# Fourteen gate tiles by Strassen's method in a hybrid attention layer on one Trainium2 core

## The chip, the core and the metric

The kernel runs on one core of a Trainium2 chip. The engines are TensorE (PE in the profile, PEld for its weight loads), VectorE (DVE), ScalarE (ACT), GpSimd (POOL) and SyncE (SP), which issues the DMA transfers here. The metric is device time in microseconds, the median over runs. Each kernel has beside it one profiled execution, from which all rows of the profile come.

## The reference

A decoder layer over 2048 positions of width 1024, with 16 meta positions ahead. One input projection makes queries, keys and values of two attention branches and four gates; both attentions are gated, projected, merged under two sigmoid gates and added to the residual.

```python
xn = rms_norm(h, norm_gain[l])
proj = xn @ w_in[l]
sb_q, sb_k, sb_v, sw_q, sw_k, sw_v, sb_z, sw_z, g_sb, g_sw = jnp.split(proj, offsets, axis=-1)
...
y_sb = (o_sb * jax.nn.silu(sb_z)) @ w_branch_sb[l]
y_sw = (o_sw * jax.nn.silu(sw_z)) @ w_branch_swa[l]
merged = jax.nn.sigmoid(g_sb) * y_sb + jax.nn.sigmoid(g_sw) * y_sw
h = h + merged @ w_out[l]
return rms_norm(h, final_norm_gain)[:, BLOCK:]
```

The change concerns `sigmoid(g_sb)` and `sigmoid(g_sw)`: 8 + 8 column tiles of 128 of the input projection.

## The kernel before

The sequence is stored in reverse and cut into four groups of 512 positions. Two halves are worked one after the other: groups 2 and 3, then groups 0 and 1. For each group the normed input lies transposed in SBUF as eight slices of 128 rows, each in two parts: `xh`, rounded to fp32r, and `xl`, the remainder. Weights are split in the same way (`weights`: `wh` by one operation of 128x1024, `wl` by a second one; both on GpSimd in the stages that matter here). A product of full accuracy is then three fp32r matmuls a slice: high by high, high by low, low by high (`gemm`, L400 to L402). So a column tile of one group is 24 matmuls of 128x128 by 128x512 into one PSUM bank.

The order on TensorE is written out by hand (`manual_schedule`); on the other engines a planner places the instructions, and each engine works its own in order. SyncE's queue is in order too. Split weights are written to DRAM in the first half and read back in the second, where they need no splitting.

A half runs through these stages:

- Projections of the sliding-window branch, with that attention woven in (`window`).
- Stick-breaking attention (`stick`), woven with gate tiles. `weave` takes the gate tiles' slices one by one and lets the attention have a share of TensorE's time after each (`ratio`). A row step makes 128 queries by up to 512 keys: two matmuls (L836), a sigmoid on ScalarE (L840), for the diagonal blocks a mask on GpSimd (L845), and a running product on VectorE (`row`, the scan of L847). Five steps later (`LT`) `turn` transposes the row on TensorE (L858) and splits it (L111 on ScalarE, L112 on VectorE), and `values` multiplies it with the values (L884). In the first half there are 8 heads, each with group 3 (4 rows) and group 2 (8 rows). With each head and group, `row` loads the queries into two buffers each of tags q1 and q2, and in the first half also a block of `x` into a buffer of tag q2, whose squares ScalarE sums for the norm of the second half (L823).
- The gate tiles that are left.

The list `gts` holds 28 gates in order: 4 for the stick-breaking z, 8 for the sliding-window z (both with silu), 8 for `g_sb`, 8 for `g_sw` (sigmoid alone, L555). Each tile's result goes to DRAM (`zs`, `zw`, `gs`, `gw`). In the first half gts 3 runs ahead of the attention, gts 4 to 24 are woven with it, and gts 25 to 27 follow, group by group. Among these last, `prep` normalises the first group of the second half into the buffers of `xh[2]` and `xl[2]`; that is possible as soon as group 2 has had its last product.

```python
rest = 25 if half == 0 else 23
cost_sb = 8 * sum(4 * (4 - g) for g in groups) * 1.31 + 16 * 0.75
ratio = cost_sb / ((rest - 4) * 10.4)
weave(tiles_by_tile(gts[4:rest], groups), side, ratio)
drain(side)
```

Buffers that matter: `tmp` (nine of 128x512), `ring_x` (four), `raw` (two weight tiles as loaded), `wh` and `wl` (three each), and PSUM tags g, z and t with two banks each.

Of the kernel before, what the change touches and what calls it, by code (L numbers as in the profile page):

```python
# [8 lines left out]
F32R = mybir.dt.float32r  # L9
I32 = mybir.dt.int32  # L10
AF = mybir.ActivationFunctionType
ALU = mybir.AluOpType
# [4 lines left out]
P = 128  # L17
D = 1024
KT = D // P
SEQ = 2048  # L20
NM = 16
GT = 512
# [10 lines left out]
ULAG = 3  # L33
AB = 6
QW = 6.0
C_SBQ, C_SBK, C_SBV, C_SWQ, C_SWK, C_SWV, C_SBZ, C_SWZ, C_GSB, C_GSW = (
    0, 512, 1024, 1536, 2560, 2688, 2816, 3328, 4352, 5376)


def f32(ap):  # L40
    return ap.bitcast(F32)
# [3 lines left out]
def tile_kernel(ctx, tc, x, xt, meta, metat, gain, w_in, w_sb, w_sw, w_out, sinks, fgain,  # L45
# [6 lines left out]
    V, A, G, T = nc.vector, nc.scalar, nc.gpsimd, nc.tensor  # L52

    def DMA(dst, src):
        nc.sync.dma_start(*(t.bitcast(F32) if t.dtype == F32R else t for t in (dst, src)))
# [6 lines left out]
    def ps(tag):  # L62
        return pp.tile([P, 512], F32, tag=tag, name="ps_" + tag, bufs={"g": 2, "z": 2, "zm": 1, "t": 2, "o": 1}[tag])
# [28 lines left out]
    gs = [[dram(f"gs{p}_{g}", [P, GT]) for g in range(4)] for p in range(8)]  # L92
    gw = [[dram(f"gw{p}_{g}", [P, GT]) for g in range(4)] for p in range(8)]
# [55 lines left out]
    def drain(*gens):  # L149
        for _ in chain(*gens):  # L150
            pass
# [6 lines left out]
    def load(c0, w=w_in):  # L158
        raw = wp.tile([P, KT, P], F32, tag="raw", name="raw", bufs=2)[:, :w.shape[2], :]
        DMA(raw, w[c0 // P])  # L160
        return raw

    def weights(c0, w=w_in, raw=None, split=split):

        if c0 in ready:
            return ready.pop(c0)
        n = w.shape[2]
        wh, wl = (wp.tile([P, KT, P], F32R, tag=t, name=t, bufs=3)[:, :n, :] for t in ("wh", "wl"))
        key = w.name, c0
        if key in kept:  # L170
            for t, k in zip((wh, wl), kept[key]):
                DMA(t, k)
            return wh, wl
        raw = load(c0, w) if raw is None else raw
        split(wh, wl, raw)
        kept[key] = [dram(f"{t}_{w.name}_{c0}", [P, n, P], F32R) for t in "hl"]
        for t, k in zip((wh, wl), kept[key]):
            if put_off is None:
                DMA(k, t)
            else:  # L180
                put_off.append((k, t))
        return wh, wl
# [145 lines left out]
    xh, xl = {}, {}  # L328

    def tmp(dt=F32, rows=P):  # L330
        return tp.tile([rows, GT], dt, tag="tmp", name="tmp", bufs=9)

    def ring_x(dt=F32):
        return tp.tile([P, GT], dt, tag="xs", name="xs", bufs=XS)
# [43 lines left out]
    def prep(g, rs):  # L378

        x_tiles(g, g % 2)  # L380
        rb = scale_rows(rs)
        for k in range(KT):
            t = ring_x()
            DMA(t, xt[g, k])
            drain(normal(g, k, t, rb))
# [175 lines left out]
    def tiles_by_tile(makes, groups, meta=False):  # L561
        for mk in makes:
            w, use, wants = mk()
            for n, g in enumerate(reversed(groups) if wants == "back" else groups):
                yield from lagged(col_tile(w, g, use, meta and wants and n == 0))

    def by_group(ts, groups):
        for g in groups:
            for w, use, _ in ts:
                yield from lagged(col_tile(w, g, use))  # L570
# [204 lines left out]
    def stick(groups, bp, sums_of={}):  # L775
# [120 lines left out]
        for s in range(n + LT + 3):  # L896
# [12 lines left out]
            while av_todo and turned[0] < s - 1:  # L909
                del turned[0]  # L910
                yield values()


    sbt = [lambda p=p, f=f: f(p) for f, p in ((sb_k, 0), (sb_k, 1), (sb_q, 0), (sb_v, 0), (sb_v, 1), (sb_q, 1),
                                              (sb_k, 2), (sb_v, 2), (sb_q, 2), (sb_k, 3), (sb_v, 3), (sb_q, 3))]
    gts = ([lambda p=p: gate(C_SBZ + p * P, zs[p], True) for p in range(4)]
# [4 lines left out]
    halves = ([2, 3], [0, 1])  # L921
# [3 lines left out]
    with (tc.tile_pool(name="start", bufs=1, side="left") as bp,  # L925
# [54 lines left out]
        raw = load(C_SBK)  # L980
# [101 lines left out]
    for half, groups in enumerate(halves):  # L1082
        with tc.tile_pool(name=f"swa{half}", bufs=1, side="left") as sp:
            m = half == 0
            vsplit[0] = True
            if not m:
                ts = [mk() for mk in sbt[:3]]
                rs = rs1
            if not m:
                prep(groups[1], rs)  # L1090
                drain(by_group(ts, groups[:1]), by_group(ts, groups[1:]))
            if m:
                late_consts()
            sw_k, sw_v, sw_q, attend, ending = window(half, groups, sp)
            q = [[lambda p=p: sw_q(p) for p in (2 * s, 2 * s + 1)] for s in range(4)]
            steps = [(s, g) for s in range(4) for g in groups]
            if m:
                (wk, use_k, _), (wv, use_v, _), (wq, use_q, _) = sw_k(), sw_v(), sw_q(0)
                hold[0] = True
                drain(col_tile(wk, g0, use_k), col_tile(wv, g0, use_v), col_tile(wq, g0, use_q, bank="z"))  # L1100
                flush(waiting)
                drain(lagged(col_tile(wk, g1, use_k, True, "o", "t")))
                hold[0] = False
                meta_k = pending[:]
                del pending[:]
                drain(col_tile(wv, g1, use_v, True, "z", "t"))
                pending.append(lambda: flush(waiting))
                back = tp.tile([P, GT], F32, tag="rb", name="back", bufs=1)
                for i in range(2):
                    sums_back.append(back[:NM, i * P:(i + 1) * P])  # L1110
                    DMA(sums_back[i], msd[i])
                hand.close()
                vsplit[0] = False
                drain(tiles_by_tile(q[0][1:], groups[:1]))
                vsplit[0] = True
                late.extend(meta_k)
                pending.append(lambda: pending.extend(held))
            else:
                drain(tiles_by_tile([sw_k, sw_v], groups), tiles_by_tile(q[0], groups[:1]))
            drain(tiles_by_tile(sbt[3:4], groups, m))  # L1120
            main = chain(*[chain(tiles_by_tile(q[s], [g]), tiles_by_tile(sbt[3 + j:4 + j], groups, m))
                           for j, (s, g) in enumerate(steps) if j], tiles_by_tile([sbt[11], *gts[:3]], groups, m))
            side = attend()
            weave(main, side, 4 * 2.15 / 20.8 * SR)
            ending.append(1)
            drain(side)
            flush_all()
        with tc.tile_pool(name=f"sb{half}", bufs=1, side="left") as bp:
            vsplit[0] = False
            next_sums = {g: sums() for g in halves[1]} if half == 0 else {}  # L1130
            side = stick(groups, bp, next_sums)
            drain(tiles_by_tile(gts[3:4], groups))
            rest = 25 if half == 0 else 23
            cost_sb = 8 * sum(4 * (4 - g) for g in groups) * 1.31 + 16 * 0.75
            ratio = cost_sb / ((rest - 4) * 10.4)
            weave(tiles_by_tile(gts[4:rest], groups), side, ratio)
            drain(side)
            if half == 0:
                t, u = (bp.tile([P, GT], F32, tag="wh", name="sum", bufs=3)[:, :8] for _ in range(2))
                for n, ssq in enumerate(next_sums.values()):  # L1140
                    V.tensor_tensor(t[:, 4 * n:4 * n + 4], ssq[:, 0], ssq[:, 1], op=ALU.add)
                rs = tp.tile([P, 8], F32, tag="rs8", name="rs", bufs=1)
                rsqrt(rs, t, tp, t=u)
                rs0, rs1 = rs[:, :4], rs[:, 4:]
        if half == 0:
            ts = [mk() for mk in gts[rest:]]
            drain(by_group(ts, groups[:1]), by_group(ts[:1], groups[1:]))
            prep(halves[1][0], rs0)
            drain(by_group(ts[1:], groups[1:]))
        else:  # L1150
            ringl = rings()
            osw = {}
            todo = [(k, g) for g in halves[0] for k in range(8)]
            for mk in gts[rest:]:
                if mk is gts[-1]:
                    with tc.manual_schedule(engines={mybir.EngineType.Activation}):
                        drain(tiles_by_tile([mk], groups))
                        A.preload_act_table_set("natural_log_exp_and_others")
                else:
                    drain(tiles_by_tile([mk], groups))  # L1160
                for k, g in todo[:4]:
                    osw[k, g] = gated(ow, zw, k, g, ringl, tmp)
                del todo[:4]
            for k, g in todo:
                osw[k, g] = gated(ow, zw, k, g, ringl, tmp)
# [51 lines left out]
```

## Time and profile before

| | us |
|---|---|
| median of 3 runs (2173.67 to 2174.96) | 2173.68 |
| the profiled execution | 2175.12 |
| its span, first to last instruction | 2173.4 |
| TensorE busy in the span | 2147.3 |
| VectorE busy | 1360.6 |
| ScalarE busy | 1010.1 |
| GpSimd busy | 374.7 |

The profile's rows have line, engine, operation, output and inputs, shapes and count; then busy time and mean time of one; then idle time of the engine ahead of them and what ended it. The slices divide the span into 40 equal parts and give busy shares in tenths. Matmuls are pipelined, so a matmul's own duration is longer than the distance to the next one; distances are what count on TensorE.

### The profile page before, as it was taken

To read this page: it belongs to the slowest core of one execution; us is meant where nothing else is said; L and a number is where in the kernel's file an instruction comes from. 1 tells how busy PE (TensorE), PEld (TensorE's weight loads), DVE (VectorE), ACT (ScalarE), POOL (GpSimd) and SP (SyncE) were. 2 spreads that over 40 slices of the span, in tenths; PEclk is the share of its full clock that TensorE was granted. 3 is DMA by queue.
4 is the path that set the end of the run, shared out by engine and by line. 5 is a ranking of instruction groups with operands and counts; after the bars stand their busy time and mean duration, and the time that the engine had idled before them with its cause. 6 is when DMAs were issued, how large, how long until landed. Compare 5 with 4: busy or idle time off the path is not lost. (4 is left out here: it accounts for less than half of the span.)

```text
span 2173.4 us, 30334 instructions
## 1 busy us (share of the span) xinstructions
PE 2147.3 (99%) x10614; PEld 1764.0 (81%) x10614; DVE 1360.6 (63%) x2133; ACT 1010.1 (46%) x2344; POOL 374.7 (17%) x486
## 2 busy tenths in 40 slices
PE   8999999999999999999999999999999999999998
PEld 6788888888888888888877888888888888787886
DVE  7787875456555343877747888878774536453453
ACT  6677774344444324776744555555553202221121
POOL 2233343322232200232210000000000232000000
PEclk9999999999999999999999999999999999999999
DMA  9745445765565464444355433333324976467532
GB/s 333 284 173 194 175 165 206 251 197 196 170 196 192 157 216 155 146 148 156 133 171 150 124 122 112 115 108 97 117 86 135 349 276 205 164 218 271 154 97 87
DMA packets 162616, 380.41 MB, mean 175 GB/s; under 512 B 23168, under 2 KB 24960, under 8 KB 162464
## 3 DMA queue, kind: packets, MB, share of 16 engines
q1 hardware_dynamic: 162464, 378.48, 51.8%
q8 instruction: 84, 1.38, 0.3%
q14 instruction: 68, 0.56, 0.1%
HBM read 237.35 MB, written 140.98 MB: 174 GB/s over the span
## 5 line engine op out<-in xcount | busy, mean ns | idle before, releaser
L400 PE MATMUL ps_g<-xh,wh 128*128 128x512 f32 x1544 | 637.5, 413 | 7.7 <-ACT xh L934 6.8
L402 PE MATMUL ps_g<-xh,wl 128*128 128x512 f32 x1544 | 607.5, 393 | 1.0 <-DVE wl L108 1.0
L401 PE MATMUL ps_g<-xl,wh 128*128 128x512 f32 x1544 | 607.2, 393 | 0.0
L847 DVE TENSOR_TENSOR_SCAN row<-row 128x512 f32<-128x512 f32 (+2 forms) x320 | 371.2, 1162 | 167.0 <-POOL row L845 96.3
L402 PEld LDWEIGHTS ps_g<-xh,wl 128*128 128x128 f32 x1544 | 290.3, 188 | 66.9 <-DVE wl L108 1.9
L400 PEld LDWEIGHTS ps_g<-xh,wh 128*128 128x128 f32 x1544 | 291.7, 189 | 54.7 <-ACT xh L934 6.8
L401 PEld LDWEIGHTS ps_g<-xl,wh 128*128 128x128 f32 x1544 | 292.0, 189 | 43.7 <-DVE xl L935 1.3
L840 ACT ACTIVATE row<-ps_z 128x512 f32<-128x512 f32 (+1 forms) x320 | 171.9, 538 | 250.9 <-PE ps_z L836 207.9
L112 DVE SCALAR_TENSOR_TENSOR wtl<-ps_t,wth 128x512 fp32r<-128x512 f32 (+1 forms) x320 | 190.0, 594 | 47.3 <-ACT wth L111 45.8
L111 ACT ACTIVATE wth<-ps_t 128x512 fp32r<-128x512 f32 (+1 forms) x320 | 170.2, 532 | 91.1 <-PE ps_t L858 89.3
L836 PE MATMUL ps_z<-kt,q 128*128 128x512 f32 (+3 forms) x640 | 185.1, 370 | 0.3 <-ACT row L840 0.3
L858 PE MATMUL ps_t<-ident,row 128*128 128x128 f32 x1088 | 171.6, 273 | 1.2 <-DVE row L847 1.2
L858 PEld LDWEIGHTS ps_t<-ident,row 128*128 128x128 f32 x1088 | 135.9, 140 | 37.3 <-DVE row L847 1.7
L845 POOL TENSOR_SCALAR_AFFINE_SELECT row<-row 128x128 f32<-128x128 f32 x128 | 45.8, 359 | 620.0 <-ACT row L840 547.6
L836 PEld LDWEIGHTS ps_z<-kt,q 128*128 128x128 f32 x640 | 118.8, 188 | 26.4 <-ACT row L840 0.8
L884 PE MATMUL ps_o<-wth,vc 128*128 128x512 f32 (+1 forms) x320 | 125.8, 393 | 1.3 <-DVE tmp L889 1.1
L555 ACT ACTIVATE tmp<-ps_g 128x512 f32<-128x512 f32 x112 | 67.0, 598 | 121.3 <-PE ps_g L402 118.8
L107 POOL TENSOR_SCALAR wh<-raw 128x1024 fp32r<-128x1024 f32 (+1 forms) x63 | 65.8, 1045 | 331.3 <-PE ps_g L401 142.8
L701 ACT ACTIVATE sc<-sc,nm 128x129 f32<-128x129 f32 x256 | 100.0, 393 | 37.9 <-DVE nm L699 37.2
L884 PE MATMUL ps_o<-wtl,vc 128*128 128x512 f32 (+1 forms) x320 | 116.9, 365 | 0.0
L108 POOL TENSOR_TENSOR wl<-raw,wh 128x1024 fp32r<-128x1024 f32 (+1 forms) x43 | 96.6, 2245 | 3.2
L616 POOL TENSOR_TENSOR tmp<-tmp 128x512 f32<-128x512 f32 (+1 forms) x37 | 48.7, 1318 | 201.9 <-DVE tmp L615 157.9
(308 smaller groups left out, 3416.8 us busy)
## 6 DMA issues: line engine op xcount, KB each, us to landing
wh<-h_in_w_in SPq DMA_DIRECT2D x66, 512.0 KB, 3.8
wl<-l_in_w_in SPq DMA_DIRECT2D x66, 512.0 KB, 4.9
raw<-in_w_in SPq DMA_DIRECT2D x50, 512.0 KB, 5.5
h_in_w_in<-wh SPq DMA_DIRECT2D x50, 512.0 KB, 2.9
l_in_w_in<-wl SPq DMA_DIRECT2D x50, 512.0 KB, 3.7
q<-qd SPq DMA_DIRECT2D x128, 128.0 KB, 3.3
vc<-vd SPq DMA_DIRECT2D x48, 256.0 KB, 3.9
kd<-tmp SPq DMA_DIRECT2D x32, 256.0 KB, 4.8
```

Of the source, the lines that this page charges most:

```text
L108: (V if vsplit[0] else G).tensor_tensor(l, src, f32(h), op=ALU.subtract)
L111: A.activation(h, acc, AF.Copy, scale=scale)
L112: V.scalar_tensor_tensor(l, acc, scale, f32(h), op0=ALU.mult, op1=ALU.subtract)
L400: T.matmul(acc, lhsT=wh[:, k, :], rhs=xh[g][:, k, :], start=k == 0, stop=False)
L401: T.matmul(acc, lhsT=wh[:, k, :], rhs=xl[g][:, k, :], start=False, stop=False)
L402: T.matmul(acc, lhsT=wl[:, k, :], rhs=xh[g][:, k, :], start=False, stop=k == KT - 1)
L701: A.activation(sc[:, hh, :], sc[:, hh, :], AF.Exp, bias=nm[:, hh:hh + 1], accum_out=den[:, hh:hh + 1])
L836: T.matmul(z[:, :w], lhsT=lq, rhs=kt[h][:, k0:k0 + w], start=t == 0, stop=t == 1)
L840: A.activation(r[:, :w], z[:, :w], AF.Sigmoid, scale=-1.0)
L847: V.tensor_tensor_scan(r[:, :w], r[:, :w], r[:, :w], last[j] if n else 1.0, op0=ALU.mult, op1=ALU.min)
L858: T.transpose(tr[:, j * P:(j + 1) * P], rows_of[h, g, n - (j > i), j][:, k0:k0 + P], ident)
L884: T.matmul(o[:, :n], lhsT=v, rhs=r, start=first and r is wh, stop=last and r is wl)
```

## The change

The gates of the last 14 tiles of `gts` (two of `g_sb`'s eight stay ordinary) leave the weave and the ordinary loop. They are taken as 7 pairs of column tiles, and each pair with both groups and both halves of the contraction forms a product of 2 by 2 blocks: weights a11, a12 (first column tile, first and second half of the contraction), a21, a22 (second column tile); inputs b11, b21 (first group), b12, b22 (second group). Strassen's method in Winograd's form needs seven block products, not eight. With s1 = a21 + a22, s2 = s1 - a11, s3 = a11 - a21, s4 = a12 - s2 and t1 = b12 - b11, t2 = b22 - t1, t3 = b22 - b12, t4 = b21 - t2 (with the signs of the code), the seven are a11 b11, s2 t2, a12 b21, s1 t1, s3 t3, s4 b22 and a22 t4. Each is 4 slices of three matmuls.

- `combined` makes t2, t3 and t4 for the whole stage, split in high and low parts, on VectorE, GpSimd and ScalarE, in a pool that takes the memory of the attention's pool. t1 stays unsplit in four `ring_x` buffers and is written over the first half of `xh[3]` and `xl[3]` (`last`) once the ordinary tiles are done.
- `pair_weights` loads and splits a pair's two weight tiles as before and makes the four sums, split as well.
- `gate_pairs` runs the seven products over six PSUM banks and adds them on VectorE with four `tmp` tiles; then the sigmoids and the transfers out. The next pair's weights are asked for ahead of each pair. `prep` of the second half's first group comes after the third product of the last pair.
- `rest` becomes 12 in the first half: gts 4 to 11 are woven with the attention (`ratio` follows), gts 12 and 13 run as ordinary tiles behind it.

```diff
+SB = 5
+FAST = 14
...
+    HK = KT // 2
+
+    def put(hl, k, t):
+        A.copy(hl[0][:, k, :], t)
+        V.tensor_tensor(hl[1][:, k, :], t, f32(hl[0][:, k, :]), op=ALU.subtract)
+
+    def combined(ga, gb, pool):
+
+        t2, t3, t4 = [tuple(pool.tile([P, HK, GT], F32R, tag=f"{n}{s}", name=f"{n}{s}") for s in "hl")
+                      for n in ("t2", "t3", "t4")]
+        t1 = (xh[gb], xl[gb])
+        firsts = []
...
+        for k in range(HK):
+            (h11, l11), (h21, l21), (h12, l12), (h22, l22) = (part(g, k + j) for g in (ga, gb) for j in (0, HK))
+            s, e, u = ring_x(), tmp(), tmp()
+            firsts.append(s)
+            V.tensor_tensor(s, h12, h11, op=ALU.subtract)
+            G.tensor_tensor(e, l12, l11, op=ALU.subtract)
+            V.tensor_tensor(s, s, e, op=ALU.add)
+            V.tensor_tensor(u, h22, s, op=ALU.subtract)
+            V.tensor_tensor(u, u, l22, op=ALU.add)
+            put(t2, k, u)
+            V.tensor_tensor(u, h21, u, op=ALU.subtract)
+            G.tensor_tensor(u, u, l21, op=ALU.add)
+            put(t4, k, u)
+        for k in range(HK):
+            (h12, l12), (h22, l22) = part(gb, k), part(gb, k + HK)
+            u, e = tmp(), tmp()
+            G.tensor_tensor(e, l22, l12, op=ALU.subtract)
+            V.tensor_tensor(u, h22, h12, op=ALU.subtract)
+            V.tensor_tensor(u, u, e, op=ALU.add)
+            put(t3, k, u)
+
+        def last():
+            for k in range(HK):
+                put(t1, k, firsts[k])
+        return t1, t2, t3, t4, last
+
+    def pair_weights(c, d, pool):
+
+        raws = [load(c0) for c0 in (c, d)]
+        whole = [weights(c0, raw=r) for c0, r in zip((c, d), raws)]
+        a11, a12, a21, a22 = (r[:, j:j + HK, :] for r in raws for j in (0, HK))
+        r1, r2, r3, r4 = (tmp().rearrange("p (k c) -> p k c", k=HK) for _ in range(4))
+        V.tensor_tensor(r1, a21, a22, op=ALU.add)
+        V.tensor_tensor(r2, r1, a11, op=ALU.subtract)
+        V.tensor_tensor(r3, a11, a21, op=ALU.subtract)
+        V.tensor_tensor(r4, a12, r2, op=ALU.subtract)
+        sums_w = {}
+        for n, r in ((2, r2), (1, r1), (3, r3), (4, r4)):
+            h, l = sums_w[n] = [pool.tile([P, HK, P], F32R, tag="s" + i, name="s" + i, bufs=SB) for i in "hl"]
+            A.copy(h, r)
+            V.tensor_tensor(l, r, f32(h), op=ALU.subtract)
...
+    def gate_pairs(ga, gb, pairs, pool, sums_x, between):
+
+        t1, t2, t3, t4, last = sums_x
+        last()
...
+        def product(a, b):
+            acc = ps("gzt"[next(banks) % 3])
+            (wh, wl), (h, l) = a, b
+            for k in range(HK):
+                T.matmul(acc, lhsT=wh[:, k, :], rhs=h[:, k, :], start=k == 0, stop=False)
+                T.matmul(acc, lhsT=wh[:, k, :], rhs=l[:, k, :], start=False, stop=False)
+                T.matmul(acc, lhsT=wl[:, k, :], rhs=h[:, k, :], start=False, stop=k == HK - 1)
+            return acc
...
+        nxt = pair_weights(pairs[0][0], pairs[0][2], pool)
+        for n, (c, cdst, d, ddst) in enumerate(pairs):
+            a11, a12, a22, s1, s2, s3, s4 = nxt
+            end = n + 1 == len(pairs)
+            if not end:
+                nxt = pair_weights(pairs[n + 1][0], pairs[n + 1][2], pool)
+            p, u, v, w = (tmp() for _ in range(4))
+            A.copy(p, product(a11, b11))
+            add(u, product(s2, t2), p)
+            add(p, product(a12, b21), p)
+            gate_out(cdst[ga], p)
+            if end:
+                between()
+            p5 = product(s1, t1)
+            add(v, p5, u)
+            add(u, product(s3, t3), u)
+            add(w, p5, u)
+            gate_out(ddst[gb], w)
+            add(v, product(s4, b22), v)
+            gate_out(cdst[gb], v)
+            add(u, product(a22, t4), u)
+            gate_out(ddst[ga], u)
...
-            rest = 25 if half == 0 else 23
+            rest = 26 - FAST if half == 0 else 23
...
-            ts = [mk() for mk in gts[rest:]]
-            drain(by_group(ts, groups[:1]), by_group(ts[:1], groups[1:]))
-            prep(halves[1][0], rs0)
-            drain(by_group(ts[1:], groups[1:]))
+            with tc.tile_pool(name="fast", bufs=1, side="left") as bp:
+                sums_x = combined(*groups, bp)
+                drain(tiles_by_tile(gts[rest:-FAST], groups))
+                places = [(C_GSB + i * P, gs[i]) for i in range(8)] + [(C_GSW + i * P, gw[i]) for i in range(8)]
+                places = places[-FAST:]
+                gate_pairs(*groups, [a + b for a, b in zip(places[::2], places[1::2])], bp, sums_x,
+                           lambda: prep(halves[1][0], rs0))
```

More of the change, by code (lines that the diff above doesn't have):

```diff
@@ L911, in stick, with part @@
                 yield values()
+    HK = KT // 2
[7 more added lines that the diff above has]
+        firsts = []
+        def part(g, k):
+            return f32(xh[g][:, k, :]), f32(xl[g][:, k, :])
+        for k in range(HK):
[22 more added lines that the diff above has]
+        return t1, t2, t3, t4, last
@@ new lines, in pair_weights @@
+    def pair_weights(c, d, pool):
[12 more added lines that the diff above has]
+            V.tensor_tensor(l, r, f32(h), op=ALU.subtract)
+        s1, s2, s3, s4 = (sums_w[n] for n in (1, 2, 3, 4))
+        (h1, l1), (h2, l2) = whole
+        return ((h1[:, :HK, :], l1[:, :HK, :]), (h1[:, HK:, :], l1[:, HK:, :]), (h2[:, HK:, :], l2[:, HK:, :]),
+                s1, s2, s3, s4)
@@ new lines, in gate_pairs, with add, gate_out @@
+    def gate_pairs(ga, gb, pairs, pool, sums_x, between):
+        t1, t2, t3, t4, last = sums_x
+        last()
+        b11, b21 = ((xh[ga][:, j:j + HK, :], xl[ga][:, j:j + HK, :]) for j in (0, HK))
+        b22 = xh[gb][:, HK:, :], xl[gb][:, HK:, :]
+        banks = iter(range(1 << 30))
+        def product(a, b):
[6 more added lines that the diff above has]
+            return acc
+        def add(t, acc, u):
+            V.tensor_tensor(t, acc, u, op=ALU.add)
+        def gate_out(dst, t):
+            A.activation(t, t, AF.Sigmoid)
+            DMA(dst, t)
+        nxt = pair_weights(pairs[0][0], pairs[0][2], pool)
[20 more added lines that the diff above has]
+            gate_out(ddst[ga], u)
```

## The prediction

> **What bounds the kernel now.** I read the busy times and slices first, then the rows of the stages that the change touches.
>
> ```profile
> PE 2147.3 (99%) x10614; PEld 1764.0 (81%) x10614; DVE 1360.6 (63%) x2133; ACT 1010.1 (46%) x2344; POOL 374.7 (17%) x486
> ...
> PE   8999999999999999999999999999999999999998
> ...
> DVE  7787875456555343877747888878774536453453
> ...
> PEclk9999999999999999999999999999999999999999
> ```
>
> TensorE has work in every slice at the full granted clock, so the time is the number of its products times their pitch, plus the few gaps. The pitch is read from two sigmoids that close neighbouring gate tiles, in ScalarE's instructions in order of time (start us, us; the first row ends the last tile before the stick-breaking rows begin):
>
> ```profile
> 397.74 0.60 ACT L555 ACTIVATE tmp<-ps_g 128x512 f32<-128x512 f32 x1 [4.84 <-PE ps_g L402]
> ...
> 749.30 0.60 ACT L555 ACTIVATE tmp<-ps_g 128x512 f32<-128x512 f32 x1 [0.87 <-PE ps_g L402]
> 754.74 0.60 ACT L555 ACTIVATE tmp<-ps_g 128x512 f32<-128x512 f32 x1 [4.84 <-PE ps_g L402]
> 760.18 0.60 ACT L555 ACTIVATE tmp<-ps_g 128x512 f32<-128x512 f32 x1 [4.84 <-PE ps_g L402]
> ```
>
> One gate tile of one group is 24 matmuls (8 slices of the contraction, 3 terms) and takes 754.74 to 760.18 = 5.44 us, or 0.2267 us a matmul. From 397.74 to 749.30 run 21 gate tiles of two groups (gts 4 to 24) with the stick-breaking attention of the first half woven in: 351.56 us, of which 21 x 10.88 = 228.5 are gates, so attention takes 123.1 us of TensorE.
>
> **The change, what it removes.** Fourteen tiles of two groups were 14 x 10.88 = 152.3 us. They become 7 pairs, each of seven products of 12 matmuls (4 slices, 3 terms): 7 x 7 x 12 x 0.2267 = 133.3 us. **Removed: 19.0 us**, 84 matmuls. The full gain counts only if TensorE never waits longer than before. Three places are new.
>
> **Place one: the attention loses cover.** The weave now has 8 gate tiles, not 21: 87.0 + 123.1 = 210.1 us, 96 row steps (8 heads, 4 and 8 rows) of 2.19 us instead of 3.66. VectorE's need is in the stretch table (sum of busy us and count per engine; before the change, first half and second half):
>
> ```profile
> 398.40:745.60 347.20, 347.20 (x1774) 286.14 (x1774) 191.68 (x243) 146.49 (x313) 98.36 (x109) 1.00 0.56 184
> 1160.00:1650.00 490.00, 488.73 (x2635) 405.94 (x2634) 398.22 (x485) 266.21 (x520) 17.55 (x60) 1.00 0.35 107
> ```
>
> The second half already runs this way: 398.22 of 490 us of VectorE (81%), with 1.3 us of TensorE idle. The first half after the change would have at most 191.68 in 210, 91%. Part of that is time in which scans stand against GpSimd, which is seen by comparing equal scans of the first half (four rows) with the second (four rows; the columns end in busy us, mean ns):
>
> ```profile
> L847 DVE TENSOR_TENSOR_SCAN row<-row 128x528 f32<-128x528 f32 x16 | 24.9, 1555 | 24.7 <-POOL row L845 15.4 <-ACT row L842 9.3
> L847 DVE TENSOR_TENSOR_SCAN row<-row 128x400 f32<-128x400 f32 x16 | 21.0, 1312 | 14.3 <-ACT row L840 10.2 <-POOL row L845 3.7
> L847 DVE TENSOR_TENSOR_SCAN row<-row 128x272 f32<-128x272 f32 x16 | 15.2, 951 | 10.8 <-ACT row L840 6.8 <-POOL row L845 3.7
> L847 DVE TENSOR_TENSOR_SCAN row<-row 128x144 f32<-128x144 f32 x16 | 10.8, 672 | 4.9 <-POOL row L845 4.5 <-ACT row L840 0.3
> ...
> L847 DVE TENSOR_TENSOR_SCAN row<-row 128x528 f32<-128x528 f32 x16 | 21.1, 1317 | 10.6 <-ACT row L842 10.6
> L847 DVE TENSOR_TENSOR_SCAN row<-row 128x400 f32<-128x400 f32 x16 | 16.8, 1049 | 3.0 <-ACT row L840 2.9
> L847 DVE TENSOR_TENSOR_SCAN row<-row 128x272 f32<-128x272 f32 x16 | 12.5, 779 | 2.9 <-ACT row L840 2.5
> L847 DVE TENSOR_TENSOR_SCAN row<-row 128x144 f32<-128x144 f32 x16 | 8.3, 516 | 2.8 <-ACT row L840 2.4
> ```
>
> They lose 71.9 - 58.7 = 13.2 us over the weight splits of 21 tiles. With 8 splits left, some 5 remain: 183 to 184 us, 87%. So VectorE does not become the bound by its sum, but little slack is left to make up a delay.
>
> One chain has its own deadline. In the first half each step from one head's group to the next also loads a block of x for its squares into the query buffers (two of them, tag q2), so the second query tile cannot be fetched ahead. ScalarE's and SyncE's rows at such a turn, then the DMA view's row for the queries (count, KB, median us to landing):
>
> ```profile
> 467.07 0.29 ACT L840 ACTIVATE row<-ps_z 128x144 f32<-128x144 f32 x1 [0.34 <-PE ps_z L836]
> 472.95 0.63 ACT L823 ACTIVATE xq<-xq 128x512 f32<-128x512 f32 x1 [1.75 <-DMA xq<-in_x]
> 485.62 0.58 ACT L840 ACTIVATE row<-ps_z 128x512 f32<-128x512 f32 x1
> ...
> 468.14 0.55 SPq L55 DMA_DIRECT2D xq<-in_x  x1
> 473.70 1.08 SPq L55 DMA_DIRECT2D q<-qd  x2
> ...
> q<-qd SPq DMA_DIRECT2D x56, 128.0 KB, 2.8
> ```
>
> Group 2 of a head ends its rows at 467.07; its buffer takes x, is squared at 472.95, and the query for the next head's group 2 is issued until 474.78 and lands about 2.8 us after its issue, 10 us after 467.07. It is first needed five steps later, at 485.62: 18.6 us before the change, about 5 x 2.19 = 10.9 us after. The margin shrinks from 8 to 1 us, at seven turns. Behind a late query TensorE stands whole, because its order is fixed by hand. I take half a microsecond a turn (3.5) and 1.5 for rows whose mask waits behind a weight split on POOL: **5 us**. Bounds: 0 (the chain just holds, as in the second half) and 28 (4 us late at each of seven turns, the third rival).
>
> **Place two: the combinations before the pairs.** They start when the attention has freed its temporaries, and two ordinary gate tiles (21.8 us) cover them. VectorE gets 10 operations for each of 4 slices, 4 more when the second group's first half is overwritten, 8 for the first pair's weights: 52, of which 4 need nothing that is late: 48. GpSimd gets 12 operations of 128x512 and the splits of two weight tiles. Their prices, from VectorE's and GpSimd's rows in order of time:
>
> ```profile
> 774.83 2.49 DVE L376 TENSOR_TENSOR xl<-xs,xh 128x512 fp32r<-128x512 f32 x4
> ...
> 749.13 1.06 POOL L107 TENSOR_SCALAR wh<-raw 128x1024 fp32r<-128x1024 f32 x1 [1.29 <-PE ps_g L401]
> 750.27 2.39 POOL L108 TENSOR_TENSOR wl<-raw,wh 128x1024 fp32r<-128x1024 f32 x1
> ...
> 824.85 1.28 POOL L616 TENSOR_TENSOR tmp<-tmp 128x512 f32<-128x512 f32 x1 [72.18 <-DVE tmp L615]
> ```
>
> VectorE: 48 x 0.62 = 29.8 us. GpSimd: 12 x 1.28 + 2 x 3.45 = 22.3 us. Counted from the end of attention, the products start at 21.8, 24.5 (needs t2 and s2), 27.2, 29.9 (t1, s1), 32.6 (t3, s3), 35.4 (s4), 38.1 (t4 and the second weight tile). If both engines ran side by side, 29.8 would meet these starts nearly everywhere: 0. But operations with two inputs in SBUF do not run beside GpSimd:
>
> ```profile
> 432.05 2.38 POOL L108 TENSOR_TENSOR wl<-raw,wh 128x1024 fp32r<-128x1024 f32 x1
> 448.93 2.40 POOL L108 TENSOR_TENSOR wl<-raw,wh 128x1024 fp32r<-128x1024 f32 x1
> ...
> 432.80 3.33 DVE L847 TENSOR_TENSOR_SCAN row<-row 128x400 f32<-128x400 f32 x2
> 449.98 0.56 DVE L112 SCALAR_TENSOR_TENSOR wtl<-ps_t,wth 128x384 fp32r<-128x384 f32 x1 [0.69 <-ACT wth L111]
> ```
>
> The two scans (widths 400 and 272) take 1.05 + 0.78 us alone and 3.33 here; the first stood until POOL was done at 434.43. The eviction at 449.98, with one input in PSUM, lost nothing. All 48 operations have two inputs in SBUF, so the other end is both engines in turn: 29.8 + 22.3 = 52.1, against 38.1 plus 2 us of early start: 12 us late. Between them I scale what was lost: 13.2 us in 21 x 3.45 = 72 us of splits with VectorE 55% busy, so about a third of GpSimd's time when VectorE always has work, 7 us: 36.8 against 32.6, plus a cast on ScalarE ahead of each remainder: **5 us**.
>
> The rule behind this stands in the Trainium skill, SBUF — State Buffer, section "Who interferes with whom": a VectorE instruction with two SBUF inputs and a GpSimd instruction that reads SBUF lock each other out for their whole length. By this rule this place costs 12, not 5; the trace agrees in the rows just shown.
>
> **Place three: the pairs themselves.** A pair has 7 x 2.72 = 19.04 us of TensorE. VectorE has 8 x 0.62 for weights and 7 evictions of 0.69: 9.8 us; GpSimd 6.9; ScalarE 9 operations of 0.6: 5.4. Six PSUM banks let the evictions come five products late, and a pair's weights are made one pair ahead. DMA: 2 raw tiles, 4 kept ones of 512 KB and 4 outputs of 256 KB, 4.2 MB in 19 us or 220 GB/s, against 184 in the stretch above. With the cover of a whole pair I count the sum at 1 us, for the first refill of the two raw buffers, behind which stand the split on GpSimd, the remainders on VectorE and then every later product; if it is gone, one raw load and split stand in each pair's way. The preparation of x for the second half moves from a cover of 4 x 2.72 = 10.9 us (two group tiles) to 5 products, 13.6 us: nothing. SyncE's queue carries the same weight and output transfers, 13 tiles' worth moved behind the attention's od and query transfers.
>
> **Sum.** 19.0 - 5 - 5 - 1 = 8 us less. The profiled execution took 2175.1 us with a span of 2173.4; it would become 2165.4 in span. Against the median of 2173.7 (1.4 below the profiled one): **2165.7 us**.
>
> **Rivals.**
> - *All of it arrives.* Second half at 81% of VectorE shows 1.3 us idle, and that is the nearest row to place one; combinations hoisted into the attention would make place two free. Against: that half runs few GpSimd operations; the first half has on most rows, splits and the x loads. 19 - 0 to 4: 2154.6 to 2159.
> - *The combinations run in turn with GpSimd.* For: the scans above. 19 - 12 - 5 - 1 = 1: 2172.7, no change. The same rule of the Trainium skill, in SBUF — State Buffer, gives this time.
> - *The query chain decides, slower.* Each turn's x load or query waits behind another transfer on SyncE, whose queue is in order. For: at such a turn the queue already stood for 6 us on queries:
>
> ```profile
> 402.81 5.94 SPq L55 DMA_DIRECT2D q<-qd  x3
> ```
>
> Against: the other turns read show 8 to 10 us for the chain. At 4 us late per turn, 28 us: 19 - 28 - 5 - 1 = -15, 2188.7. It turns the sign from (19 - 6) / 7 = 1.9 us per turn.
> - *The removed matmuls don't show as time:* shorter accumulations of 12 with a bank change after each cost more than 0.2267 a matmul. At 0.23 us per product (one matmul), 49 products give back 11 us, against the 8 of the sum: 2176.7.
>
> **How the numbers follow.** Forecast 0.45 (its own range 2160 to 2171), all arrives 0.15, in turn 0.18, query chain 0.17, product overhead 0.05. About 0.2%, 4.3 us, can be told from no change here, so faster is below 2169.3 and slower above 2178.0. Faster: 0.38 + 0.15 + 0.05 + 0.02 = 0.60; same: 0.07 + 0.10 + 0.02 = 0.19; slower: 0.03 + 0.17 + 0.01 = 0.21. The range goes from all of it, 2155, up to 2180, which leaves out most of the query case and little else.
>
> **What would show it.** Right: 84 fewer gate matmuls, the attention stretch of the first half near 215 us, idle TensorE before the second and fifth products of the first pair, steady 2.72 us spacing from the second pair on. Wrong: more than 10 us of TensorE waiting on queries at the turns (third rival), or VectorE operations of 1.3 us and more beside GpSimd with over 10 us of idle in the first pair (second), or waits on weights in every pair.

## The result, and the profile after

| | before | after |
|---|---|---|
| median of the runs, us | 2174.02 (2173.67 to 2174.96) | 2207.04 (2203.91 to 2208.15) |
| span of the profiled execution, us | 2173.4 | 2206.4 |
| TensorE busy in the span, us | 2147.3 | 2136.7 |

The time is 1.0149 times that of before (95% interval 1.0131 to 1.0166): 33 us slower, where 8 us faster was forecast. (Before has one execution more here than in the table further up.) The page of the kernel after, busy times and slices:

```profile
PE 2136.7 (97%) x10530; PEld 1748.7 (79%) x10530; DVE 1476.5 (67%) x2282; ACT 1034.6 (47%) x2395; POOL 405.7 (18%) x498
...
PE   8999999989959999999999999999999999999998
...
PEclk9999999999989999999999999999999999999999
```

TensorE has 84 instructions fewer (10614 before) and is 10.6 us less busy, yet the span is longer: TensorE now stands. In the row of slices two places have turned (a slice is 55 us): the 8 in the ninth slice, in the attention, and above all the 5 in the twelfth, behind it. The table of stretches shows these stages (busy us and count of TensorE, weight loads, VectorE, ScalarE and GpSimd; then granted clock, DMA share, GB/s):

```profile
397.70:627.80 230.10, 212.76 (x1169) 172.74 (x1168) 170.75 (x242) 126.89 (x289) 61.16 (x84) 1.00 0.50 160
627.80:640.70 12.90, 11.34 (x49) 8.75 (x47) 11.74 (x14) 3.28 (x5) 8.12 (x6) 1.00 0.31 112
640.70:664.40 23.70, 0.03 (x1) 0.00 (x0) 23.67 (x22) 5.28 (x10) 16.42 (x10) 0.56 0.11 44
...
685.00:800.00 115.00, 115.00 (x499) 93.33 (x498) 77.98 (x91) 32.16 (x55) 44.84 (x24) 1.00 0.64 229
```

The first row is the attention with its 8 woven tiles: 17.3 us without work on TensorE, where the row of before showed none. The second and third are the two ordinary tiles: TensorE stands for 23.7 us in one piece, while VectorE is busy for all of it. The last is the pairs: not a moment of waiting. The view of waits names what TensorE waited for (us in total, times, longest), from the attention to the pairs:

```profile
PE ps_g L402 <- ACT tmp L557: 23.7, 1, 23.7
PE ps_o L886 <- DVE tmp L891: 9.1, 13, 1.3
PE ps_t L860 <- DVE wtl L114: 3.8, 4, 1.5
PE ps_zm L871 <- ACT row L844: 3.0, 4, 0.8
PE ps_g L402 <- DVE tmp L559: 1.6, 1, 1.6
```

(Lines of before are two further down in this kernel: L555 is now L557, L889 is L891.) There is no wait on a query or on a DMA. In the attention the largest is that for the single PSUM bank of `o`, the sum over values: when a head's group is done, its bank must be read out before the next one's first product, and there is no second bank. ScalarE copies one half, and VectorE then adds the other to it. VectorE's row for this add in before, then ScalarE's, VectorE's and TensorE's rows at one turn of after:

```profile
510.74 0.68 DVE L889 TENSOR_TENSOR tmp<-ps_o,tmp 64x512 f32<-64x512 f32 x1 [1.22 <-ACT tmp L888]
...
491.28 0.58 ACT L890 COPY tmp<-ps_o 64x512 f32<-64x512 f32 x1 [0.20 <-PE ps_o L886]
...
490.46 2.33 DVE L849 TENSOR_TENSOR_SCAN row<-row 128x512 f32<-128x512 f32 x2
492.71 0.53 DVE L114 SCALAR_TENSOR_TENSOR wtl<-ps_t,wth 128x384 fp32r<-128x384 f32 x1
493.16 0.67 DVE L891 TENSOR_TENSOR tmp<-ps_o,tmp 64x512 f32<-64x512 f32 x1
...
493.88 0.50 PE L886 MATMUL ps_o<-wth,vc 128*128 128x512 f32 x1 [1.26 <-DVE tmp L891]
```

In the row of before VectorE is ready and waits for the copy (L888, now L890). In after the copy is done at 491.86, and the add starts at 493.16, behind two scans and a split; TensorE waits for 1.26 us. The long wait in the table is for a sigmoid that has not read its bank of `ps_g`. The instructions in order of time around it (start us, us; VectorE, GpSimd, ScalarE, TensorE):

```profile
649.36 1.75 DVE L940 TENSOR_TENSOR tmp<-tmp,xl 128x512 f32<-128x512 f32 x1
...
662.54 0.68 DVE L950 TENSOR_TENSOR tmp<-tmp 128x512 f32<-128x512 f32 x1
...
647.18 5.05 POOL L948 TENSOR_TENSOR tmp<-xl 128x512 f32<-128x512 f32 x3
...
629.91 0.60 ACT L557 ACTIVATE tmp<-ps_g 128x512 f32<-128x512 f32 x1
663.78 0.59 ACT L557 ACTIVATE tmp<-ps_g 128x512 f32<-128x512 f32 x1
...
664.42 0.79 PE L402 MATMUL ps_g<-xh,wh 128*128 128x512 f32 x1 [23.69 <-ACT tmp L557]
665.44 0.63 PE L404 MATMUL ps_g<-xh,wl 128*128 128x512 f32 x1
665.87 0.63 PE L402 MATMUL ps_g<-xh,wh 128*128 128x512 f32 x1
667.56 0.40 PE L403 MATMUL ps_g<-xl,wh 128*128 128x512 f32 x1
667.79 0.40 PE L404 MATMUL ps_g<-xh,wl 128*128 128x512 f32 x1
```

Between the sigmoids at 629.91 and 663.78 lies the making of the combinations. They write their intermediates into `tmp`, 16 tiles of them, and there are nine buffers, given out in program order. The gate tile's sigmoid comes behind them in the program, so its buffer is the seventeenth, and comes free when eight of the 16 have been released: read from the rows, the eighth is released by the operation at 662.54, at 663.2, and the sigmoid follows. The rows also show VectorE: operations of one shape take 0.68 us, or 1.75 when GpSimd works at the same time (647.18 to 652.23).

The account, against the execution before: attention 230.1 against 8 x 10.88 + 123.1 = 210.1, **+20** (17.3 of them standing; the other 2.7 weren't traced); the two ordinary tiles 627.8 to 676.7, 48.9 against 21.8, **+27** (23.7 + 1.6 of waits, some 1.4 at half clock); the pairs 136.9 against 133.3, **+3 to 4**; removed −19. That makes 31 to 32 of the 33; the rest wasn't traced.

### The profile page after: what moved, and what is told of

Same layout as the page of the kernel before. It is cut to its first block, busy times and chain, and to the rows that moved or that the text cites. A ratio compares the mean times of both kernels' runs of the same rounds, so it can differ in the third digit from the quotient of the medians.

```text
span 2206.4 us, 30448 instructions
## 1 busy us (share of the span) xinstructions
PE 2136.7 (97%) x10530; PEld 1748.7 (79%) x10530; DVE 1476.5 (67%) x2282; ACT 1034.6 (47%) x2395; POOL 405.7 (18%) x498
## 4 chain that ended last, share of the span: by engine, by line
PE 55%; DMA 2%; DVE 1%; ACT 1%; issue 0%; SPq 0%; POOL 0%; DVEq 0%; ACTq 0%; POOLq 0%
PE ps_g L402 7%; PE ps_g L404 7%; PE ps_g L403 7%; PE ps_o L886 4%; PE ps_z L838 4%; PE ps_t L860 4%; PE ps_o L741 1%; PE ps_z L695 1%; PE ps_g L226 1%; PE ps_g L225 1%; PE ps_g L224 1%; PE ps_z L226 1%; PE ps_z L224 1%; PE ps_z L225 1%; PE ps_t L226 1%; PE ps_t L224 1%
## 5 line engine op out<-in xcount | busy, mean ns | idle before, releaser
L402 PE MATMUL ps_g<-xh,wh 128*128 128x512 f32 x1320 | 542.5, 411 | 33.3 <-ACT tmp L557 23.7
L404 PE MATMUL ps_g<-xh,wl 128*128 128x512 f32 x1320 | 519.5, 394 | 0.6 <-DVE wl L110 0.6
L403 PE MATMUL ps_g<-xl,wh 128*128 128x512 f32 x1320 | 518.7, 393 | 0.3 <-DVE xl L378 0.2
L849 DVE TENSOR_TENSOR_SCAN row<-row 128x512 f32<-128x512 f32 (+2 forms) x320 | 357.6, 1121 | 104.3 <-POOL row L847 47.1
L402 PEld LDWEIGHTS ps_g<-xh,wh 128*128 128x128 f32 x1320 | 249.8, 189 | 76.2 <-ACT tmp L557 24.6
L404 PEld LDWEIGHTS ps_g<-xh,wl 128*128 128x128 f32 x1320 | 248.4, 188 | 56.6 <-DVE wl L110 1.1
L403 PEld LDWEIGHTS ps_g<-xl,wh 128*128 128x128 f32 x1320 | 249.9, 189 | 40.8 <-DVE xl L1048 1.3
L886 PE MATMUL ps_o<-wth,vc 128*128 128x512 f32 (+1 forms) x320 | 130.4, 408 | 10.3 <-DVE tmp L891 10.2
L557 ACT ACTIVATE tmp<-ps_g 128x512 f32<-128x512 f32 x84 | 50.1, 597 | 84.2 <-PE ps_g L404 81.1
L263 ACT CAST ringl<-gt 128x512 fp32r<-128x512 f32 x32 | 19.9, 621 | 130.8 <-DVE gt L261 122.9
```

The costliest lines, as they stand in the source:

```text
L402: T.matmul(acc, lhsT=wh[:, k, :], rhs=xh[g][:, k, :], start=k == 0, stop=False)
L403: T.matmul(acc, lhsT=wh[:, k, :], rhs=xl[g][:, k, :], start=False, stop=False)
L404: T.matmul(acc, lhsT=wl[:, k, :], rhs=xh[g][:, k, :], start=False, stop=k == KT - 1)
L849: V.tensor_tensor_scan(r[:, :w], r[:, :w], r[:, :w], last[j] if n else 1.0, op0=ALU.mult, op1=ALU.min)
L886: T.matmul(o[:, :n], lhsT=v, rhs=r, start=first and r is wh, stop=last and r is wl)
```

## The experiments

**Two places taken apart.** The first run keeps seven pairs and gives the combinations other buffers than `tmp` (`short` takes them from the tags sh and sl, five each, which afterwards hold the pairs' split sums of weights); the second keeps the thin cover of the attention and has no Strassen at all.

```diff
-            s, e, u = ring_x(), tmp(), tmp()
+            s, e, u = ring_x(), short('l'), short('h')
...
-            u, e = tmp(), tmp()
+            u, e = short('h'), short('l')
```

> The changed kernel, with the sums e and u of the combinations taken from the weight-sum buffers instead of the nine shared tmp buffers; the same work. Theory A (the gate tiles' sigmoids stood behind the combinations for a tmp buffer, since buffers of one tag are handed out in program order): the one TensorE wait of 24 us on the sigmoid goes, and with it the 2 to 3 us at a lower granted clock behind it; what is left there is the lockstep of VectorE and GpSimd, 5 to 12 us ahead of the second to fifth product of the first pair: 2207 - 26 + 5 to 12 = 2186 to 2193. Rival B (the wait is the combinations' own length, and the sigmoid only ends it): the wait moves to the first pair at full length, 2203 or more.

Measured: 2203.3 us, 1.013 (1.0101 to 1.016): 4 us less than after, not 14 to 21, as the second theory had it. The waits of TensorE in that kernel:

```profile
PE ps_z L994 <- ACT sh L974: 12.8, 1, 12.8
...
PE ps_g L994 <- ACT tmp L557: 5.6, 1, 5.6
```

The wait has moved from the ordinary tile to the first pair, 18.4 us. The buffers were what the sigmoid waited for, but behind them stands the length of the combining: 631 to 677, 46 us of VectorE. Why it takes 46 shows in the rows of VectorE and GpSimd of the same kernel:

```profile
642.33 1.77 DVE L943 TENSOR_TENSOR ch<-ch,xl 128x512 f32<-128x512 f32 x1
...
645.72 0.68 DVE L941 TENSOR_TENSOR xs<-xs,cl 128x512 f32<-128x512 f32 x1
...
640.12 5.13 POOL L951 TENSOR_TENSOR cl<-xl 128x512 f32<-128x512 f32 x3
```

While GpSimd runs (640.12 to 645.25) each VectorE operation takes 1.77 us, and each of GpSimd's three 1.7; while it is silent, 0.68. Both engines lose: on these rows they work in turn, one operation each, and what is lost is not "a third" of GpSimd's time. The rule of the Trainium skill, SBUF — State Buffer, section "Who interferes with whom" (such instructions lock each other out for their whole length), holds here: 1.77 is one own turn and one of the other's.

```diff
-            rest = 25 if half == 0 else 23
+            rest = 12 if half == 0 else 23
...
-            ts = [mk() for mk in gts[rest:]]
+            drain(tiles_by_tile(gts[rest:25], groups))
+            ts = [mk() for mk in gts[25:]]
```

> The kernel before with only the weave changed: 8 gate tiles woven with the first half's attention in place of 21, the other 13 as ordinary tiles behind it; no Strassen, the same matmuls. Theory A (the attention's own chain over single PSUM banks is bare without gate tiles): 20 us more, 2194, with TensorE waits on the o bank's add (some 10 us), on the transposes' eviction and on the zm bank, and none on queries. Rival B (the 20 us come from the combinations or the pair weights reaching into the attention): 2174 to 2178. Rival C (the prediction's query chain): 20 us more, but with TensorE waits on query loads.

Measured: 2196.58 us, 1.0099 (1.007 to 1.0129), against 2175.71 for before beside it: 21 us slower with the same products as before, only 13 tiles of cover moved behind the attention. Its waits in the attention:

```profile
PE ps_o L884 <- DVE tmp L889: 9.1, 13, 1.4
PE ps_t L858 <- DVE wtl L112: 3.4, 4, 1.5
PE ps_zm L869 <- ACT row L842: 3.0, 4, 0.8
```

These are the changed kernel's waits almost to the tenth. So the attention's +20 belongs to the cover alone, and no query is among its releasers: the third rival's chain is out.

**Four pairs in place of seven.** Eight fast tiles (12 woven, 4 ordinary ahead of the pairs), with the buffers of the first run.

```diff
-FAST = 14
+FAST = 8
...
-            rest = 26 - FAST if half == 0 else 23
+            rest = 24 - FAST if half == 0 else 23
```

> Four pairs in place of seven and four ordinary tiles ahead of them in place of two, with the combinations' own buffers of the first experiment: 12 gate tiles stay in the attention's weave, 2.6 us a row step. Removed matmuls: 4 x 2.72 = 10.9 us. Theory A (cover): the attention's stall falls from 20 us to about 8, and 43.5 us of ordinary tiles hide the 36 us of combinations: 2174 - 10.9 + 8 + 1 = 2172. Rival B (the combinations hold up the pairs whatever the cover): 2180 or more.

Measured: 2198.59 us, 1.0109 (1.0079 to 1.0138). Theory A, 2172 us, fell. The waits where the combinations are made:

```profile
PE ps_g L402 <- ACT tmp L557: 13.7, 3, 9.0
```

ScalarE's rows at the end of the longest:

```profile
705.18 0.62 ACT L919 CAST t3h<-ch 128x512 fp32r<-128x512 f32 x1 [4.34 <-DVE ch L953]
...
706.91 1.08 ACT L557 ACTIVATE tmp<-ps_g 128x512 f32<-128x512 f32 x2
```

Four ordinary tiles, 43.5 us of cover, and still 13.7 us: the sigmoids (L557) stand in ScalarE's queue behind casts (L919), and the casts wait for VectorE operations that GpSimd's slow down. The next run takes GpSimd's three operations to VectorE, which gives VectorE 12 operations more.

```diff
-            G.tensor_tensor(e, l12, l11, op=ALU.subtract)
+            V.tensor_tensor(e, l12, l11, op=ALU.subtract)
...
-            G.tensor_tensor(u, u, l21, op=ALU.add)
+            V.tensor_tensor(u, u, l21, op=ALU.add)
...
-            G.tensor_tensor(e, l22, l12, op=ALU.subtract)
+            V.tensor_tensor(e, l22, l12, op=ALU.subtract)
```

> The third experiment (four pairs, four ordinary tiles ahead) with the 12 GpSimd operations of the combinations on VectorE. Theory A (VectorE's operations with two SBUF inputs stand still while GpSimd runs, which the planner doesn't reckon with, and so ScalarE's casts stand ahead of the gates' sigmoids): VectorE's operations there return from 1.8 to 0.6 to 0.7 us, the 13.7 us of TensorE wait on the sigmoids fall to 3 or less, 2198.6 becomes 2182 to 2187. Rival B (the casts on ScalarE, or 60 VectorE operations of 0.62, are too much in any order): 10 us of wait stay, 2194 or more.

Measured: 2182.48 us, 1.0037 (1.0026 to 1.0049): 16 us less, as the first theory had it, with more work on the engine that was the bound. The waits in the same place:

```profile
PE ps_g L404 <- POOL wl L110: 2.0, 1, 2.0
PE ps_z L994 <- ACT sh L974: 0.5, 1, 0.5
PE ps_z L996 <- DVE sl L975: 0.4, 1, 0.4
```

13.7 us have become 2.9. With seven pairs and two ordinary tiles the same edit was not enough:

> The first experiment (seven pairs, own buffers, two ordinary tiles ahead) with the 12 GpSimd operations of the combinations on VectorE. Theory A (full exclusion of the two engines): the work ahead of the first pair's second to seventh product is 48 x 0.62 + 12 x 0.62 + 2 splits of 3.45 = 44 us in place of 52: 2203.3 becomes 2194 to 2199, still with 8 us or more of wait at the first pair. Rival B (a third of GpSimd's time is lost, as the prediction took it): VectorE gets 7.4 us more and loses 7 less, no change, 2202 to 2205.

Measured: 2201.01 us in two runs that lie 11 us apart (1.0058 to 1.0181), which doesn't tell the theories apart. In the profiled one TensorE waited 9.5 us on a remainder of t3 and 3.3 us on weights at the first pair.

**The bank of `o`.** Where a head's group is done, ScalarE copies one half of the bank and VectorE adds the other from PSUM. With two copies on ScalarE the bank is free without VectorE. On the thin weave, on four pairs, and on the kernel before alone:

```diff
-                t = tmp(rows=64)
+                t, u = tmp(rows=64), tmp(rows=64)
                 A.copy(t, o[64:128])
-                V.tensor_tensor(t, o[0:64], t, op=ALU.add)
+                A.copy(u, o[0:64])
+                V.tensor_tensor(t, u, t, op=ALU.add)
```

> The thin weave of the second experiment (no Strassen), with the o bank freed by two ScalarE copies of its halves; the add then runs from SBUF. 16 more copies on ScalarE, 9.6 us. Theory A (the attention stands at its one o bank while VectorE's queue reaches the add): TensorE's waits on o fall from 9 us to under 3 and the time from 2196.6 to 2188 to 2191. Rival B (the attention is held by ScalarE and VectorE as a whole): the waits move to the transposes and the zm bank, 2195 or more.

> The fifth experiment with the two ScalarE copies of the fourth as well. Theory A: both gains add up, the fifth's time less the 4 us that TensorE waits on the o bank there: 2178 to 2183, still not below the kernel before, because 12 woven tiles leave 6 us of other waits in the attention. Rival B: the copies take from ScalarE what they give, equal to the fifth.

> The kernel before with the two copies for the o bank alone. Theory A (with 21 tiles woven the o bank is never waited for): within 2 us of the kernel before; what the copies bring in the other runs is cover that the change took away. Rival B (the copies are a gain of their own): 2170 or less.

| | without | with two copies | against before |
|---|---|---|---|
| thin weave | 2196.58 | 2185.36 | 1.0048 (1.0032 to 1.0064) |
| four pairs | 2182.48 | 2173.24 | 0.9994 (0.9983 to 1.0006) |
| before | 2174.83 | 2172.17 | 0.9985 (0.9976 to 0.9995) |

The waits of the thin weave with two copies:

```profile
PE ps_t L858 <- DVE wtl L112: 4.5, 5, 1.5
...
PE ps_o L884 <- ACT tmp L889: 0.9, 3, 0.4
```

The wait for `o` goes from 9.1 to 0.9 us, and the time falls by 11.2, where 6 to 9 were expected. Not all of it is cover: the second half runs the same code. ScalarE's table load ahead of the second half's gate sigmoids (L555) is a mark between the halves. In the profiled executions it stands at 1115.5 us in before and at 1135.6 in the thin weave, 20 us later; with two copies it stands at 1126.6. So the one bank's turn was 9 of the 20 us that the cover hid. The rest of the gain lies behind the mark. The kernel before gains 2.7 us, between what its two theories expected, and there the mark hardly moves (1115.5 and 1115.4): with full cover TensorE never waits on `o` in the first half, and in the second it did so for 1.1 us in all. What is left on the thin weave is the transposes' read-out (`wtl`) and, unchanged at 3.0 us, the other single bank (`zm`). The four pairs gained 9.2 us, more than was expected; their mark moves by 6.5 (1121.5 to 1115.0), and the rest is again in the second half.

**How many pairs.** With all three edits, and with the weight splits of the pairs' stage on ScalarE and VectorE so that GpSimd is silent there, six, seven and five pairs:

```diff
+                hsplit[0] = vsplit[0] = True
                 sums_x = combined(*groups, bp)
...
+                hsplit[0] = vsplit[0] = False
```

> Six pairs, four ordinary tiles ahead of them, 8 woven; combinations from their own buffers and on VectorE, two copies for the o bank, and from the combinations on the weights split on ScalarE and VectorE, so that GpSimd is silent there. Removed 6 x 2.72 = 16.3 us; the attention with 8 woven tiles costs the 10.5 us of the fourth experiment. Theory A (both losses are settled by these causes): 2174.8 - 16.3 + 10.5 + 0 to 3 = 2169 to 2172, below the kernel before. Rival B (more waits at the pairs): 2175 or more.

> The same with seven pairs and only two ordinary tiles ahead, as in the change. Removed 19.0; attention 10.5; 60 combining operations and the weights' ten (8 sums, 2 remainders of 1.22) are 45 us of VectorE against starts at 21.8 to 38.1 us. Theory A (VectorE's own sum is what is left at place two): 5 to 10 us of wait at the first pair: 2171 to 2176. Rival B (without GpSimd nothing waits there): 2166 to 2168.

> The same with five pairs and 10 woven tiles. Removed 13.6 us; the attention's loss lies between the fourth experiment's 10.5 (8 tiles) and the seventh's 5.4 (12 tiles), 8. Theory A: 2174.8 - 13.6 + 8 + 0 to 3 = 2169 to 2172, equal to six pairs within 2 us, since a pair brings 2.7 us and its two tiles' cover costs about as much. Rival B (the cover costs clearly more or less than that): the two differ by over 3 us.

| pairs | woven, ordinary tiles | us | against before |
|---|---|---|---|
| 7 | 8, 2 | 2186.46 | 1.0048 (1.0033 to 1.0063) |
| 6 | 8, 4 | 2175.62 | 1.0003 (0.9994 to 1.0013) |
| 5 | 10, 4 | 2165.95 | 0.9962 (0.9948 to 0.9976) |

Five pairs are faster than both kernels, by 8.9 us against before. Two copies alone bring before 2.7 of these, so against before with two copies the five pairs are worth 6.2. They were expected at 2169 to 2172, equal to six, and came 3 below. Six were expected at 2169 to 2172 and missed that by 4, seven at 2171 to 2176 and missed by 10. In the kernel with five pairs, the stretches of the attention, the combining and the pairs (columns as above):

```profile
390.00:640.00 250.00, 245.81 (x1330) 203.25 (x1329) 188.77 (x260) 143.23 (x317) 61.13 (x85) 1.00 0.56 179
640.00:700.00 60.00, 60.00 (x265) 49.32 (x264) 51.41 (x79) 28.06 (x44) 0.00 (x0) 1.00 0.62 222
700.00:790.00 90.00, 90.00 (x396) 73.34 (x395) 53.08 (x79) 33.30 (x51) 1.53 (x4) 1.00 0.68 238
```

TensorE stands 4 us in the attention and not at all behind it. By the count, five pairs remove 5 x (21.76 − 19.04) = 13.6 us; the span is 10.3 shorter, of which 7.7 lie ahead of the mark between the halves (1107.8 against 1115.5). Two tiles less of cover make a sixth pair, and cost more than its 2.7 us: six pairs show this wait in the attention, and the stretches around it (columns as above), then TensorE's instructions:

```profile
570.00:575.00 5.00, 3.10 (x9) 2.62 (x10) 5.00 (x7) 2.28 (x5) 1.50 (x2) 0.61 0.98 324
575.00:580.00 5.00, 5.00 (x19) 3.69 (x19) 2.44 (x5) 2.71 (x6) 0.31 (x1) 0.70 0.29 92
```

```profile
571.90 0.90 PE L860 MATMUL ps_t<-ident,row 128*128 128x128 f32 x3 [2.79 <-DVE wtl L114]
573.03 0.63 PE L403 MATMUL ps_g<-xl,wh 128*128 128x512 f32 x1
573.46 0.63 PE L404 MATMUL ps_g<-xh,wl 128*128 128x512 f32 x1
578.07 0.40 PE L886 MATMUL ps_o<-wtl,vc 128*128 128x512 f32 x1
578.31 0.39 PE L838 MATMUL ps_z<-kt,q 128*128 128x512 f32 x1
```

A wait of 2.8 us, and then matmuls of 128x512 start 0.43 us apart, not 0.23, until about 578: the clock costs some 2.5 us on top of the wait. What delayed `wtl` there (an x block for the squares, then a weight cast and its remainder ahead of it) is read from the order of instructions and wasn't tried by itself. With seven pairs and two ordinary tiles, the first pair waits again:

```profile
PE ps_z L995 <- ACT sh L975: 7.0, 1, 7.0
```

So two ordinary tiles, 21.8 us, don't cover the combining even without GpSimd; four do.

## Why the prediction was wrong, step by step

- **Removed, 19.0:** right. 84 matmuls are gone, and in the kernel after the seven pairs ran without a wait. That the matmuls wouldn't show as time (last rival) is out as a cost per product, below.
- **Place one, attention: 5 said, 20 measured, inside its bounds of 0 to 28 by luck, for the upper one was made of late queries.** The failed step is "The second half already runs this way", which took VectorE's share of time (81% there, 87% forecast) for the measure of slack. VectorE was busy 170.75 of 230.1 us and TensorE stood all the same: what counts is the delay between a bank's last product and its read-out, with one bank of `o` and of `zm`, and a read-out that queues behind scans on VectorE. The first half turns `o` after 4 or 8 rows, 16 times in 230 us, where the second half does so 16 times in some 490; with 21 woven tiles more products stood between. The thin weave shows the whole price without the change, and two copies take 9 of its 20 us away. The query chain, on which 3.5 of the 5 were put, cost nothing.
- **Place two, combinations: 5 said, 27 measured, outside its bounds of 0 to 12.** Two steps failed. "So about a third of GpSimd's time" scaled a loss from a stage in which VectorE was idle for 45% of the time; for two engines that both always have work the rows just above that sentence already showed the answer, one operation standing for the other's whole length, and the end "both engines in turn", 52 us, was the one to take (the first run: 46 us). And even that end's price of 12 supposed that the two ordinary tiles run as cover. They didn't: their sigmoids waited for a buffer of `tmp`, and with that mended, in ScalarE's queue behind casts. The second rival had the right mechanism, at less than half its price.
- **Place three, pairs: 1 said, 3 to 4 measured.** The refill of the raw buffers, for which the 1 stood, makes TensorE wait nowhere. What is more is the pitch, TensorE's rows in the last pair of the kernel after:

```profile
802.48 0.39 PE L992 MATMUL ps_g<-xl,sh 128*128 128x512 f32 x1
...
804.58 0.39 PE L992 MATMUL ps_g<-xl,sh 128*128 128x512 f32 x1
805.28 0.40 PE L992 MATMUL ps_z<-t3l,sh 128*128 128x512 f32 x1
805.97 0.39 PE L992 MATMUL ps_z<-t3l,sh 128*128 128x512 f32 x1
...
812.93 0.40 PE L992 MATMUL ps_g<-t4l,wh 128*128 128x512 f32 x1
```

  15 slices of three matmuls in 10.45 us are 0.232 us a matmul, against 0.2267. A pair inside the stage, from one first matmul to the next (696.31 to 715.75), is 19.44 us against 19.04, or 2.8 us on seven; the sum took the pitch of the gate tiles for that of the pairs. A slice across a change of bank (804.58 to 805.28) is no longer than one inside a product (805.28 to 805.97): the last rival's cost per product isn't there.
- **Preparation of x at nothing:** right; TensorE waits 0.2 us on it.
- **Sign and range:** the range ended at 2180 because both large errors were taken as alternatives. They add: 20 + 27 + 3 − 19 is 31 of the 33.

## What to carry to other kernels

When work that covers a latency chain is made cheaper or moved away, price the chain by its single buffers and the queue in which each read-out stands, not by the busy share of an engine; the quick test is to move the cover alone. For element-wise work with two SBUF inputs, VectorE and GpSimd are one engine in this kernel, and giving GpSimd a share made both wait (16 us back when it was taken out). New work that borrows a common pool or stands in an in-order queue ahead of a short read-out makes that read-out as late as itself, and the covering work with it.

## What the runs showed of the hardware

- **A wait of 2.8 us was enough to halve the clock.** The Trainium skill, TensorE: Matmul & The Clock Gate, section "What's actually happening", says that the clock falls to half after at least one idle window of about 3.4 us and rises after a busy one. The wait of 23.7 us agrees (0.43 us spacing at 665.44, 0.23 at 667.56, 3.1 us after its end). The wait of 2.79 us with six pairs is shorter than that window and still brought half clock for about 6 us, so a few us of idle are dearer than they look. The waits of up to 1.5 us in the attention of the kernel after left the granted clock at 1.00.
- **The pitch of one matmul shape isn't fixed.** 0.2267 us in the gate tiles of before, 0.232 in the last pair of after, both at a granted clock of 1.00. In the pairs it goes by the product: in the first six, the 12 matmuls of s3 t3 take 2.72 us each time (687.98 to 690.70 in the first), which is the pitch of before, and those of s1 t1 2.81 (685.17 to 687.98). It repeats from pair to pair, so it isn't chance; what sets it wasn't tried.
